# Moving all tiles of a DMA-bound matmul kernel to multiples of 512 B in SBUF

## The chip, the cores and the metric

One core of one Trainium2 chip. The metric is the device time of one execution in microseconds, median of several; a profiled execution gives the trace, whose span runs from the first to the last instruction and is some 1.9 us shorter than the time. Runs that a ratio compares ran on the same chip in alternating rounds, and all of them were in the fast state (no run was over 1.5% above the fastest of its kernel). A ratio is the mean time of one kernel's runs over the mean of the other's of the same rounds, so it is not quite the ratio of the medians beside it.

## The reference

```python
batch, m, k, n = 16, 512, 512, 512          # a: [16, 512, 512], b: [16, 512, 512], float32
def reference(a, b):
    return np.matmul(a.transpose(0, 2, 1), b).astype(np.float32)
```

Each execution reads 33.55 MB and writes 16.78 MB.

## The kernel before

Two batches make a pair; there are 8 pairs. A partition takes 8 rows of K, which lie one after another in HBM: an input tile is 128 partitions x 16 KB, loaded as one run of 16 KB for each partition. An output tile holds two runs of 8 KB for each partition. One issuing engine (SP) queues all 16 loads and then 8 stores. A mark is a write of one element after a piece of work, which raises the semaphore that another engine waits for.

```python
x_ts = [pool.tile([P, R, M], f32, name=f"x{j}") for j in range(NX)]        # 4 input tiles, 16 KB a partition
abf_ts = [pool.tile([P, RV, M], bf, name=f"abf{v}") for v in range(V)]     # 2 + 2 bf16 tiles, 4 KB
bbf_ts = [pool.tile([P, RV, N], bf, name=f"bbf{v}") for v in range(V)]
o_ts = [pool.tile([P, G, T, N], f32, name=f"o{j}") for j in range(NO)]     # 7 output tiles, 16 KB
dve_done = pool.tile([1, 2 * pairs], f32, name="dve_done")                 # marks
act_done = pool.tile([1, pairs], f32, name="act_done")
# ... semaphores ...
for n in range(2 * pairs):
    if n >= NX:
        nc.sync.wait_ge(s_in, n - NX + 1)
    nc.sync.dma_start(x_ts[n % NX][:], in_v[n % 2][n // 2]).then_inc(s_x[n % NX], 16)
for i in range(pairs - 1):
    nc.sync.wait_ge(s_out, i + 1)
    nc.sync.dma_start(out_v[i], o_ts[i % NO][:]).then_inc(s_o if i else s_o0, 16)
# ... DVE casts x to bf16 and sets a mark, PE multiplies, ACT copies PSUM to o and sets a mark ...
# ... the last store is issued after all this ...
```

In the compiled program the first input tile starts at byte 16512 of a partition, which is 128 B past a multiple of 512 B. Since all tiles ahead of the marks are multiples of 512 B long, each of them is 128 B off.

## Time and profile before

| what | before |
|---|---|
| time, median of 3 | 124.13 us (123.99 to 124.22) |
| span | 122.2 us |
| DMA share of the span | 97.6% of 16 engines |
| PE, DVE, ACT busy | 62.9, 38.0, 31.8 us |

The lines of the profile stand in the prediction below, with how to read each. Two measures are used throughout. The views show GB/s in a stretch of the span. Finer, the trace records when each of the 16 DMA engines raises a transfer's semaphore; I call the mean of the 16 times the landing (the prediction's times of landings are those of the last of the 16), and the spacing of successive landings is the pace of the queue. A transfer of a whole tile is always 2.097 MB. A packet is one run that one DMA engine moves, here of 16, 8 or 2 KB, and the trace has its start and duration.

### The profile page before, as it was taken

What the parts mean: (1) busy time and instruction counts of PE and PEld (TensorE: products, weight loads), DVE (VectorE), ACT (ScalarE), POOL (GpSimd) and SP (SyncE); (2) the same over time, 40 slices, a digit from 0 to 9 for tenths busy, and PEclk for the clock granted to TensorE, in tenths of its full rate; (3) what the DMA queues carried; (4) which work ended last, traced back from release to release, by engine and by line L of the source; (5) the groups of instructions that cost most, each with busy time, mean ns of one, the idle gap of its engine ahead of it and who ended that gap; (6) DMA issues with size and microseconds to landing.
All of it is one profiled execution on the core that took longest, in us unless ns stands there. A gap on an engine that the chain in (4) does not pass through costs nothing. (4 is left out here: it accounts for less than half of the span.)

```text
span 122.2 us, 1261 instructions
## 1 busy us (share of the span) xinstructions
PE 62.9 (51%) x512; PEld 35.9 (29%) x512; DVE 38.0 (31%) x48; ACT 31.8 (26%) x41; POOL 0.2 (0%) x4
## 2 busy tenths in 40 slices
PE   0000099989669749969919987955970000000000
PEld 0000044546346314536605545624630000000000
DVE  0012560784194092474456248409000000000000
ACT  4000000380930830191480065092084000000000
POOL 0000000000000000000000000000000000000000
PEclk9999999999999976999996899999999655555555
DMA  4899999999999999999999999999999999999993
GB/s 97 376 440 429 440 435 429 429 429 429 429 429 429 429 429 429 424 435 418 429 424 429 429 429 424 429 400 429 429 427 429 429 427 429 424 429 429 427 429 166
DMA packets 4480, 50.33 MB, mean 412 GB/s; under 512 B 384, under 2 KB 384, under 8 KB 384
## 3 DMA queue, kind: packets, MB, share of 16 engines
q1 hardware_dynamic: 4480, 50.33, 97.6%
HBM read 33.55 MB, written 16.78 MB: 412 GB/s over the span
## 5 line engine op out<-in xcount | busy, mean ns | idle before, releaser
L101 PE MATMUL ps<-bbf,abf 64*128 64x512 bf16 x512 | 62.9, 404 | 27.9 <-PEq L96 27.9
L101 PEld LDWEIGHTS ps<-bbf,abf 64*128 64x128 bf16 x512 | 35.9, 114 | 54.4 <-issue 38.3
L119 ACT COPY o<-ps 128x1024 f32<-128x1024 f32 x32 | 30.1, 1026 | 60.2 <-PE ps L101 60.2
L80 DVE CAST abf<-x 128x2048 bf16<-128x2048 f32 x16 | 19.6, 1224 | 27.0 <-PE ps L101 18.2
L80 DVE CAST bbf<-x 128x2048 bf16<-128x2048 f32 x16 | 19.6, 1225 | 20.7 <-DMA x<-in_b_dram 20.7
L124 ACT ACTIVATE act_done<-act_done 1x1 uint32<-1x1 uint32 x8 | 1.6, 196 | 0.0
L119 ACT ACT_TABLE_LOAD x1 | 1.3, 1283 | 0.9 <-SPq L62 0.9
L86 DVE MEMSET dve_done<- 1x1 f32 x16 | 0.9, 59 | 0.0
L146 POOL MEMSET const-bfloat16-1.0<- 128x1 bf16 x1 | 0.1, 102 | 0.0
L146 POOL MEMSET const-uint8-127<- 128x1 uint8 x1 | 0.1, 102 | 0.0
L146 POOL MEMSET const-float32-0.0<- 128x1 f32 x1 | 0.1, 99 | 0.2 <-issue 0.2
L146 POOL MEMSET const-float32-1.0<- 128x1 f32 x1 | 0.1, 99 | 0.0
## 6 DMA issues: line engine op xcount, KB each, us to landing
x<-in_a_dram SPq DMA_DIRECT2D x8, 2048.0 KB, 12.2
x<-in_b_dram SPq DMA_DIRECT2D x8, 2048.0 KB, 16.0
out_dram<-o SPq DMA_DIRECT2D x8, 2048.0 KB, 30.8
```

Of the source, the lines that this page charges most:

```text
L80: nc.vector.tensor_copy(out=(bbf_ts if n % 2 else abf_ts)[v][:], in_=x_ts[n % NX][:, v * RV:(v + 1) * RV, :],).then_inc(s_cast, 1)
L86: nc.vector.memset(dve_done[:, n:n + 1], 0.0).then_inc(s_in, 1)
L101: mm = nc.tensor.matmul(ps_ts[g][h][:, t % 2, :], a_m[:, t], bbf_ts[v][rows, r, :], start=(v == 0 and r == 0), stop=(v == V - 1 and r == R ...
L119: ev = nc.scalar.copy(out=o_ts[i % NO][:, g, 2 * h:2 * h + 2, :], in_=ps_ts[g][h][:])
L124: nc.scalar.memzero(act_done[:, i:i + 1]).then_inc(s_out, 1)
L146: nc = _bacc.Bacc("TRN2", target_bir_lowering=False, num_devices=1)
```

## The change

The intent is to have all input and output tiles start at multiples of 512 B. The two small tiles of marks become one tile of 384 B at the front, which puts the first input tile at byte 16896 and every tile behind it at a multiple of 512 B.

```diff
+    done = pool.tile([1, 96], f32, name="done")
+    dve_done, act_done = done[:, 0:2 * pairs], done[:, 2 * pairs:3 * pairs]
     x_ts = [pool.tile([P, R, M], f32, name=f"x{j}") for j in range(NX)]
     abf_ts = [pool.tile([P, RV, M], bf, name=f"abf{v}") for v in range(V)]
     bbf_ts = [pool.tile([P, RV, N], bf, name=f"bbf{v}") for v in range(V)]
     o_ts = [pool.tile([P, G, T, N], f32, name=f"o{j}") for j in range(NO)]
-    dve_done = pool.tile([1, 2 * pairs], f32, name="dve_done")
-    act_done = pool.tile([1, pairs], f32, name="act_done")
```

## The prediction

> **What bounds the kernel now.** I read the slices of the page first, then the queue's total, then the groups and the waits, then the timeline for a rate that can be read off to 0.1%. The slices of the page of the kernel before:
>
> ```profile
> span 122.2 us, 1261 instructions
> ...
> DMA  4899999999999999999999999999999999999993
> GB/s 97 376 440 429 440 435 429 429 429 429 429 429 429 429 429 429 424 435 418 429 424 429 429 429 424 429 400 429 429 427 429 429 427 429 424 429 429 427 429 166
> DMA packets 4480, 50.33 MB, mean 412 GB/s; under 512 B 384, under 2 KB 384, under 8 KB 384
> ## 3 DMA queue, kind: packets, MB, share of 16 engines
> q1 hardware_dynamic: 4480, 50.33, 97.6%
> ```
>
> From the third slice (6 us) to the last but one every slice is full and moves about 429 GB/s. No stretch in the middle has the DMA engines waiting for anything. The other rows of the same page:
>
> ```profile
> PE 62.9 (51%) x512; PEld 35.9 (29%) x512; DVE 38.0 (31%) x48; ACT 31.8 (26%) x41; POOL 0.2 (0%) x4
> ...
> x<-in_a_dram SPq DMA_DIRECT2D x8, 2048.0 KB, 12.2
> x<-in_b_dram SPq DMA_DIRECT2D x8, 2048.0 KB, 16.0
> out_dram<-o SPq DMA_DIRECT2D x8, 2048.0 KB, 30.8
> ```
>
> No compute engine is busy for more than 51% of the span. The 24 transfers are of 2.097 MB each; each takes 12 to 31 us from issue to landing because others stand ahead of it in the queue. The waits say who pays:
>
> ```profile
> DVE bbf L80 <- DMA x<-in_b_dram: 20.7, 8, 3.6
> ...
> SPq L157 <- DMA out_dram<-o: 27.7, 1, 27.7
> ```
>
> The casts wait for loads, and at the end all that is left is a 27.7 us wait for stores. The chain of waits ends with compute at 93 us and accounts for only 8% of the span; that is because it can't follow a queue of transfers, and it must not be read as "nothing bounds it". The timeline gives the rate of the loads, since the cast of each b tile starts as its load lands:
>
> ```profile
> 13.64 1.23 DVE L80 CAST bbf<-x 128x2048 bf16<-128x2048 f32 x1 [3.65 <-DMA x<-in_b_dram]
> ...
> 82.18 1.23 DVE L80 CAST bbf<-x 128x2048 bf16<-128x2048 f32 x1 [3.35 <-DMA x<-in_b_dram]
> ```
>
> Between these two are 14 loads: (82.18 - 13.64) / 14 = 4.896 us for one load, 428 GB/s. The last load lands at 82.2 us, so the first two thirds of the span are 16 loads and the rest 8 stores: 82.2 + 8 x 4.89 = 121.3, plus 0.9 us to the end of the span. The semaphore records of the trace give the same more finely: loads land 4.894 us apart (8.75 to 82.16 us, 15 steps), stores 4.886 us apart (91.94 to 116.37 us, 5 steps). The kernel is bound by 24 x 4.89 = 117.4 us of DMA in one queue, and 4.9 us lie around it (start of the first transfer at 2.0 us, some 1.9 us lost on the first packets, which took up to 1.75 us each, and 0.9 us at the end).
>
> **What the Trainium skill says.** (1) The page "DMA: Bandwidth & Descriptors", section "Where 436 GB/s comes from": 16 ports x 32 B x 850 MHz = 435.2 GB/s. At that rate a transfer takes 2,097,152 B / 435.2 GB/s = 4.819 us. The trace shows 4.89, 98.5% of it, so it agrees as a ceiling. (2) The same page, "How a descriptor splits into AXI transactions": data goes in transactions of 256 B and beats of 32 B, and a transaction must start at a multiple of 256 B, so a run that starts off it pays for beats it doesn't use. In the compiled program of the kernel before, four constants of 32 B slots stand ahead of the first input tile, which begins at byte 16512 = 32 x 512 + 128. All input and output tiles are multiples of 512 B long, so every one begins 128 B past such a boundary: 4 beats. (3) The same page, "Why small descriptors are slow (HBM only)": about 3 cycles of overhead for each packet. The packet records behind the page's third section fit well: loads are 2048 packets of 16 KB with a median near 611 ns (12 to 30 us), stores 2048 packets of 8 KB at 309 ns. In cycles of 1/850 MHz = 1.176 ns, 611 ns is 519 = 512 beats + 4 + 3, and 309 ns is 263 = 256 + 4 + 3. That is just what a start 128 B off would cost, though a fixed overhead of 7 cycles for whatever other reason would fit as well. (4) The page "SBUF — State Buffer", section "Operand start alignment", demands only a start at a multiple of the element size and says that it is about legality and not speed. Nothing there makes 512 B a threshold.
>
> **The change part by part.** (a) One tile of 384 B takes the place of two of 64 and 32 B and moves to the front. 16512 + 384 = 16896 = 33 x 512, so all input, bf16 and output tiles move by 384 B and begin at multiples of 512 B. No instruction, wait, transfer or byte is added or removed; the marks are written by the same 16 memsets of 59 ns and 8 activations of 196 ns, into different columns. Both engines now write the same tile, but inside a section with hand-made semaphores, where I expect no new wait. Cost: 0. (b) Casts, matmuls and copies read and write at moved addresses. Their durations shouldn't change, and they aren't on the path: the last store is issued at 93.1 us and its packets start after 116.4 us, 23 us of slack. Worth: 0. (c) Loads: each of the 16 engines carries 8 packets of 16 KB per load, 8 x 16 = 128 in all. If the writes into SBUF lose 4 beats each, it is 128 x 4 x 1.176 ns = 0.60 us. (d) Stores: 16 packets of 8 KB per engine and store, 16 x 8 = 128: again 128 x 4.7 ns = 0.60 us.
>
> Whether (c) and (d) are really paid is seen better from the spacing of the landings than from the packets' durations, since neighbouring packets may overlap. One transfer has 131,072 B per engine, 4096 beats. A load takes 4.894 us = 4160 cycles: 64 over the beats. A store takes 4.886 us = 4153 cycles: 57 over. With 3 cycles for each data packet, a store's 16 packets take 48, and 9 remain for its semaphore packet (9 ns in the records, about 8 cycles). So the stores' spacing is explained without any misalignment, and their 309 ns must overlap by some 4 cycles. A load's 8 packets with the same overhead take 24 + 9 = 33, and 31 cycles are left: 4 for each packet. So the loads seem to pay for the misalignment and the stores seem not to. This is where I chose: (c) in full, (d) not. Sum: 124.13 - 0.60 = 123.53 us, 123.5.
>
> **The rivals.** *Nothing changes:* the 31 cycles of the loads come from reading HBM, or are part of a 16 KB packet whatever its address, and the skill's rule is written for reads, where the loads' reads from HBM are presumably aligned already. For: loads and stores are within 0.2% of each other though one writes SBUF and the other reads it. Against: the overheads come out at whole packets' 4 beats. Time: 124.1. *Both pay:* stores read SBUF, which is the side that the rule describes, and 309 ns fits it; with the overlap gone the spacing of stores could fall by 4 beats as well. Time: 122.9. *More than the sum:* a 512 B boundary could matter for some other reason, in the first packets as well (1.9 us lost there). But at the ceiling of 435.2 GB/s the 24 transfers would take 115.7 us, 1.7 us less than now, which is 1.4%: more than 2% (below 121.65 us) would need a rate above that ceiling or a start without loss. Nothing in the trace speaks for it. *Slower:* the two engines' marks in one tile bring a wait, or the aligned tiles collide in SBUF. With compute 23 us ahead at the end, and a queue that holds about three loads ahead (12 to 16 us from issue to landing, 4.9 us each), a wait of some 100 ns on a mark would be hidden. Time: 124.1 to 124.3.
>
> **Range and chances.** I give the loads alone 0.42, nothing 0.30, both 0.18, more 0.06, slower 0.04. Executions spread by 0.1 us either way. The range from 122.8 to 124.25 us holds the first three with their spread, which is more than 8 in 10; the middle is 123.5. Faster by over 2% has 0.04, slower by over 2% 0.01, the rest is within 2%: 0.95.
>
> **What would show it.** If (c) is right, packets of 16 KB fall from 611 to about 606 ns, the casts of b tiles stand 4.856 us per load apart rather than 4.896, the last load lands near 81.6 rather than 82.2 us, and the slices between 10 and 80 us show about 432 rather than 429 GB/s. If (d) is paid after all, stores stand 4.85 us apart rather than 4.886; if packets of 8 KB go from 309 to 305 ns with the spacing unchanged, the overlap is what hid it. If "nothing changes" is right, both spacings stay to 0.005 us and the seven cycles are a packet's own. The groups of casts, matmuls and copies should keep their means (1225, 404, 1026 ns), and the wait for stores at the end its 27.7 us within 0.5. I'm wrong about the kind of the effect if the span changes by more than 1.7 us, if the gain lies ahead of the first landing (8.8 us), or if a new wait on the marks shows.

## The result, and the profile after

| | before | after |
|---|---|---|
| time, median of 6 | 124.10 us (123.99 to 124.44) | 123.89 us (123.68 to 124.08) |
| ratio | | 0.9978, 95% interval 0.9963 to 0.9994 |
| span of the profiled run | 122.2 us | 121.9 us |

The change is worth 0.22%, 0.27 us. That is clear of noise; the sum of the prediction had said 0.60 us.

The slices and the queue on the page of the changed kernel:

```profile
span 121.9 us, 1261 instructions
...
GB/s 108 360 430 430 436 430 430 430 430 430 430 430 430 430 430 436 430 430 430 430 430 430 430 430 430 436 390 428 428 430 430 430 428 430 430 430 428 428 428 175
...
q1 hardware_dynamic: 4480, 50.33, 97.6%
```

In the loads (slices 4 to 26) most slices have 430 where they had 429; slice 27, where loads give way to stores, has 390 against 400. Everything else is as it was: the same packets, the same bytes, casts of 1225 ns, copies of 1026 ns, no new wait. The wait of the issuing engine for the last stores, in the view of its waits:

```profile
SPq L159 <- DMA out_dram<-o: 27.8, 1, 27.8
```

The timeline has the casts that start when the first and the last b tile land:

```profile
13.67 1.23 DVE L82 CAST bbf<-x 128x2048 bf16<-128x2048 f32 x1 [3.60 <-DMA x<-in_b_dram]
...
81.79 1.23 DVE L82 CAST bbf<-x 128x2048 bf16<-128x2048 f32 x1 [3.34 <-DMA x<-in_b_dram]
```

(81.79 - 13.67) / 14 = 4.866 us for a load, where it was 4.896. So 14 loads gained 0.42 us, but the end came only 0.3 us earlier. The view of busy time by stretch shows where the rest went. Its columns are the stretch, its length, the busy time of the five compute engines (with instructions), the granted TensorE clock, the DMA engines' share and GB/s. Before:

```profile
10.00:64.00 54.00, 39.89 (x320) 22.09 (x320) 25.17 (x32) 19.09 (x25) 0.00 (x0) 0.97 1.01 429
...
78.00:82.00 4.00, 3.02 (x29) 1.73 (x24) 0.83 (x1) 2.70 (x3) 0.00 (x0) 1.00 0.98 414
...
100.00:120.00 20.00, 0.00 (x0) 0.00 (x0) 0.00 (x0) 0.00 (x0) 0.00 (x0) 0.50 1.01 428
```

After:

```profile
10.00:64.00 54.00, 39.69 (x322) 22.09 (x324) 25.51 (x33) 19.10 (x25) 0.00 (x0) 0.97 1.01 431
...
78.00:82.00 4.00, 2.64 (x26) 1.43 (x21) 0.66 (x2) 3.08 (x4) 0.00 (x0) 1.00 0.98 403
...
100.00:120.00 20.00, 0.00 (x0) 0.00 (x0) 0.00 (x0) 0.00 (x0) 0.00 (x0) 0.50 1.01 429
```

The loads are faster, the end of the loads is slower (403 against 414 GB/s), the late stores are the same. The packet records explain the middle line: before, no 16 KB packet after the start of the kernel lasted over 625 ns; after, 11 packets between 78.6 and 80.5 us lasted 646 to 1064 ns. The shortest of the other packets did not become shorter: they last 611 ns in both, though before they strayed up to 624 (mean 613.8) and now nearly all are at 611.

My theory at this point: each packet that goes to or from SBUF off a boundary costs some 4 cycles, the loads' part of it is gained, and part of that is given back where loads turn into stores. The rivals: the two profiles differ by chance; or what counts is bytes or the 512 B boundary rather than packets; or aligned output tiles slow the stores.

### The profile page after: what moved, and what is told of

Its sections match the earlier page's. It is cut to its first block, busy times and chain, and to the rows that moved or that the text cites. A ratio compares the mean times of both kernels' runs of the same rounds, so it can differ in the third digit from the quotient of the medians.

```text
span 121.9 us, 1261 instructions
## 1 busy us (share of the span) xinstructions
PE 62.5 (51%) x512; PEld 35.8 (29%) x512; DVE 38.0 (31%) x48; ACT 31.8 (26%) x41; POOL 0.2 (0%) x4
## 5 line engine op out<-in xcount | busy, mean ns | idle before, releaser
L121 ACT COPY o<-ps 128x1024 f32<-128x1024 f32 x32 | 30.1, 1026 | 59.8 <-PE ps L103 59.8
L82 DVE CAST bbf<-x 128x2048 bf16<-128x2048 f32 x16 | 19.6, 1225 | 20.8 <-DMA x<-in_b_dram 20.8
L126 ACT ACTIVATE done<-done 1x1 uint32<-1x1 uint32 x8 | 1.6, 196 | 0.0
L88 DVE MEMSET done<- 1x1 f32 x16 | 0.9, 59 | 0.0
```

Of the source, the lines that this page charges most:

```text
L82: nc.vector.tensor_copy(out=(bbf_ts if n % 2 else abf_ts)[v][:], in_=x_ts[n % NX][:, v * RV:(v + 1) * RV, :],).then_inc(s_cast, 1)
L88: nc.vector.memset(dve_done[:, n:n + 1], 0.0).then_inc(s_in, 1)
L121: ev = nc.scalar.copy(out=o_ts[i % NO][:, g, 2 * h:2 * h + 2, :], in_=ps_ts[g][h][:])
L126: nc.scalar.memzero(act_done[:, i:i + 1]).then_inc(s_out, 1)
```

## The experiments

### Both kernels again, and each half of the change alone

`before_again` and `after_again` are the two kernels unedited. `x_only` puts 384 B of marks ahead of the input tiles and 128 B ahead of the output tiles; `o_only` puts the 384 B between the bf16 tiles and the output tiles. (In `x_only` the bf16 tiles move along with the input tiles; no DMA touches them.)

```diff
 # x_only, against the kernel before
+dve_done = pool.tile([1, 96], f32, name="dve_done")
 x_ts = [...]                                          # now at 0 mod 512
 ...
+act_done = pool.tile([1, 32], f32, name="act_done")
 o_ts = [...]                                          # still at 128 mod 512
-dve_done = pool.tile([1, 2 * pairs], f32, name="dve_done")
-act_done = pool.tile([1, pairs], f32, name="act_done")
```

```diff
 # o_only, against the kernel before
 x_ts = [...]                                          # still at 128 mod 512
 ...
+act_done = pool.tile([1, 96], f32, name="act_done")
 o_ts = [...]                                          # now at 0 mod 512
 dve_done = pool.tile([1, 2 * pairs], f32, name="dve_done")
-act_done = pool.tile([1, pairs], f32, name="act_done")
```

> The kernel before, unedited, for a second profile. If the spacings of the landings are properties of the kernel, loads land 4.895 us apart and stores 4.887 us apart within 0.004 us, the 16 KB packets again last 611 to 619 ns with a mean of 613.8, and the ratio is 1.000 within 0.002. If the two profiles at hand differ by chance, loads or stores shift by 0.01 us or more here.

> The changed kernel, unedited, for a second profile. If the loads' gain is real: loads 4.862 us apart within 0.004 us, every 16 KB packet at 611 ns. If the stores' loss (4.896 us apart against 4.887) comes from the alignment, it is there again; if it is chance, stores are at 4.887 to 4.890. If the slow packets of 650 to 1060 ns at 78.6 to 80.5 us belong to the change they come again there; if not, the last load lands near 81.6 us and the span is near 121.7. Ratio 0.9978 by the earlier rounds, 0.996 if the slow packets were chance.

> Only the input tiles begin at multiples of 512 B; the output tiles begin 128 B past one as before. Loads alone matter: loads 4.862 us apart, stores 4.887, ratio 0.9955 to 0.998, at least as fast as the changed kernel. If the output tiles' alignment were what costs the stores 9 ns each, this is 0.07 us faster than the changed kernel; if alignment does nothing and the profiles differ by chance, 4.894 and a ratio of 1.000.

> Only the output tiles begin at multiples of 512 B; the input tiles stay 128 B past one. If only loads pay for the offset: loads 4.895 us apart, stores 4.887, ratio 1.000 within 0.001. If aligned output tiles slow the stores: stores 4.896, ratio 1.0006. If stores pay for the offset too (the second rival of the prediction): stores 4.85, ratio 0.9975.

Measured, five rounds on one chip, with the landings of each profile (us, the first two kernels' earlier profiles ahead):

```
kernel        time    ratio (95%)               14 steps, load 1 to 15   last load   last load to last store
before                                          68.516                   4.896       39.096
before_again  124.04  0.9997 (0.9984 to 1.0010) 68.519                   4.896       39.091
o_only        124.02  0.9997 (0.9984 to 1.0010) 68.519                   4.896       39.099
after                                           68.053                   5.010       39.219
after_again   123.89  0.9983 (0.9970 to 0.9996) 68.055                   5.080       39.223
x_only        123.87  0.9988 (0.9975 to 1.0001) 68.053                   4.975       39.226
```

The view by stretch of the two halves, first `x_only`, then `o_only`:

```profile
10.00:64.00 54.00, 39.35 (x322) 22.20 (x324) 25.41 (x33) 18.36 (x24) 0.00 (x0) 0.97 1.01 432
...
78.00:82.00 4.00, 4.00 (x40) 2.56 (x36) 1.42 (x2) 1.46 (x2) 0.00 (x0) 1.00 0.97 403
```

```profile
10.00:64.00 54.00, 39.00 (x320) 22.71 (x320) 25.09 (x32) 19.08 (x25) 0.00 (x0) 0.97 1.01 430
...
78.00:82.00 4.00, 4.00 (x40) 2.36 (x38) 1.23 (x1) 1.25 (x2) 0.00 (x0) 1.00 0.98 414
```

The profiles of each class agree to a few nanoseconds, so nothing here is chance except the size of the last load's delay. The six fall into two classes, and what sorts them is the input tiles alone. With aligned inputs 14 steps of loads take 0.465 us less (4.862 against 4.895 us a load in the steady part; the 4.862 is a mean of steps that repeat in fours, from 4.84 to 4.89 us, which was not looked into), the last load takes 0.08 to 0.18 us more, and from there to the last store it takes 0.13 us more. The sum, -0.465 + 0.126 (mean) + 0.127 = -0.21 us, is what the times show (-0.15 to -0.27; the interval of `x_only` just takes in no change). The loss in the stores does not come from the output tiles: with only those aligned nothing changes at all, and with only the inputs aligned the loss is whole. My expectation of 4.887 us per store for `x_only` was wrong. That loss sits in the first stores: before, their first steps are 4.878, 4.861 and 4.881 us, after, 4.907, 4.900 and 4.899; from the fifth on both stand near 4.89 to 4.90. (Here the first step is that from the first store to the second.)

### Small packets: loads of 2 KB

The saving is small because there are few packets. If it is one of packets, eight times as many must show eight times as much. Each input tile is loaded by two transfers, of its even and its odd rows, so that every row is a run of 2 KB; both operands are permuted alike and the result stays correct. `ld2k_off` has this on the kernel before, `ld2k_on` on the changed kernel.

```diff
-nc.sync.dma_start(x_ts[n % NX][:], in_v[n % 2][n // 2]).then_inc(s_x[n % NX], 16)
+for w in range(2):
+    nc.sync.dma_start(
+        x_ts[n % NX][:, w * 4:(w + 1) * 4, :], in_v[n % 2][n // 2][:, w::2, :]
+    ).then_inc(s_x[n % NX], 16)
 ...
-nc.vector.wait_ge(s_x[n % NX], 16 * (n // NX + 1))
+nc.vector.wait_ge(s_x[n % NX], 32 * (n // NX + 1))
```

> Loads cut into packets of 2 KB: each input tile comes by two transfers, of the even and of the odd rows, so that a row of 2 KB is a run of its own (both operands alike, so the sums are the same). Tiles 128 B past a multiple of 512 B. 64 packets per engine and load where there were 8. With 3 cycles of overhead and 4 beats for the offset each: 64 x (64 + 3 + 4) = 4544 cycles and some 16 for two semaphore packets, 5.36 us per load. If the offset's cost is one of bytes and not of packets, 64 x 67 + 32 + 16 = 4336 cycles, 5.10 us.

> The same with all tiles at multiples of 512 B. If each packet saves the 3.5 to 4 beats that the 16 KB packets saved: 64 x 67 + 16 = 4304 cycles, 5.06 us per load, 0.26 to 0.30 us less than with the offset, and 4.2 to 4.8 us over the 16 loads. If the saving is one of bytes: 0.03 us per load and 0.5 us in all, as in the change.

To find the boundary and the law, three more kernels differ from `ld2k_on` only in the size of the marks' tile, which puts all tiles at 64, 192 or 256 B past a multiple of 512 B (448, 576 or 128 B in place of 384). All five are slower than the kernel before (ratios 1.028 to 1.065), since a load now has eight times the packets; they are compared with each other.

> Loads in packets of 2 KB, all tiles 64 B past a multiple of 512 B. Aligned it was 5.13 us per load (both halves), at 128 B 5.42. If the offset costs the beats between the boundary and the start, 2 for 64 B: 5.28 us per load, 2.2 us of span over the aligned one (130.0 us). If it costs one more transaction whatever the offset: 5.42 us, as at 128 B (132.2 us).

> The same, all tiles 256 B past a multiple of 512 B. If the boundary that counts is 256 B, as the skill's page has it: 5.13 us per load, 127.8 us, as aligned to 512 B. If it is 512 B: 5.42 us per load or more, 132.2 us or more.

> Loads in packets of 2 KB, all tiles 192 B past a multiple of 512 B. At 64 and 128 B the span was 132.1 us, at 0 and 256 B 127.8 us. If each packet that starts off a multiple of 256 B costs the same whatever the distance: 5.42 us per load, 132.1 us. If 192 B costs 6 beats: 5.57 us per load, 134.4 us.

The view by stretch, first `ld2k_on` (0 B past), then `ld2k_at256`, then `ld2k_off` (128 B), `ld2k_at64`, `ld2k_at192`:

```profile
10.00:80.00 70.00, 50.82 (x400) 29.58 (x402) 31.94 (x42) 22.89 (x30) 0.00 (x0) 0.93 1.05 409
```

```profile
10.00:80.00 70.00, 47.90 (x410) 28.43 (x412) 32.23 (x42) 22.91 (x30) 0.00 (x0) 1.00 1.05 409
```

```profile
10.00:80.00 70.00, 51.24 (x384) 27.51 (x384) 29.18 (x38) 20.81 (x27) 0.00 (x0) 0.90 1.05 387
```

```profile
10.00:80.00 70.00, 50.10 (x384) 27.75 (x384) 29.17 (x38) 22.31 (x29) 0.00 (x0) 0.93 1.05 387
```

```profile
10.00:80.00 70.00, 50.49 (x384) 27.94 (x384) 29.17 (x38) 22.91 (x30) 0.00 (x0) 0.93 1.05 387
```

The last column takes one of two values: 409 GB/s at 0 and 256 B, 387 at 64, 128 and 192 B. The times and the spacing of the half tiles' landings say the same more finely:

```
B past 512   time     half tile
0            127.78   2.566 us
256          127.91   2.566
64           132.11   2.711
128          132.18   2.710
192          132.17   2.710
```

The kernels at 0 and 128 B ran on one chip, those at 256 and 64 B on another, that at 192 B (two runs) on a third; the half tiles' spacing agrees to 1 ns within each group. So 4.40 us (3.4%) are lost or gained by the start address alone. A half tile has 32 packets per engine: (2.710 - 2.566) / 32 = 4.5 ns each, 3.8 of the cycles of 1.176 ns that the prediction counts in. The packets' own durations agree: 84.0 ns on average at 0 and 256 B, 88.2 to 88.8 ns at the other three. For the 16 KB packets it is (4.895 - 4.862) / 8 = 4.1 ns, 3.5 cycles. The saving is one of packets; saving by bytes is refuted. The boundary is 256 B; 512 B as such has no effect. And the cost doesn't grow with the distance from the boundary: 64 and 192 B cost what 128 B costs, where a cost by unused beats would have given 130.0 and 134.4 us. A run of 2 KB that starts off a boundary touches 9 blocks of 256 B in place of 8, whatever the distance. That one block more is a fit to these numbers, not a thing that a record shows.

These five kernels also repeat, on three other chips, the loss in the stores (of 8 KB packets here as before): from the last load to the last store it is 39.22 us at 0 and 256 B and 39.10 to 39.11 at 64, 128 and 192 B.

### Small packets: stores of 2 KB

`st2k_off` and `st2k_on` are the kernel before and the changed one with output rows dealt to the partitions in another order, so that a store's runs are of 2 KB (64 packets per engine and store in place of 16).

```diff
-out_v = out.rearrange("(pair g) (c t) n -> pair c g t n", g=G, t=T)
+out_v = out.rearrange("(pair g) (t c) n -> pair c g t n", g=G, t=T)
 ...
-a_m = abf_ts[v][rows, r, :].rearrange("p (c t) -> p t c", t=T)
+a_m = abf_ts[v][rows, r, :].rearrange("p (t c) -> p t c", t=T)
```

> Stores cut into packets of 2 KB (output row t x 128 + c instead of 4 c + t sits in partition c, the columns of the first operand are taken to match, so the result is the same); loads as before. Tiles 128 B past a multiple of 512 B. 64 packets per engine and store where there were 16: with 3 cycles each, 64 x 67 + 9 = 4297 cycles, 5.06 us per store, if the offset costs stores nothing; 64 x 71 + 9 = 4553 cycles, 5.36 us, if it costs them 4 beats. Loads 4.895 us apart.

> The same with all tiles at multiples of 512 B. If stores pay nothing for the offset, stores stand as far apart as with it, within 0.02 us, and only the loads gain, 0.5 us in all. If they pay 4 beats for each packet, each store is 0.30 us shorter, 2.4 us over the 8. If an aligned output tile makes stores slower by packet, they are 9 x 4 = 36 ns longer each.

The stretch of the late stores, off and on:

```profile
95.00:120.00 25.00, 0.00 (x0) 0.00 (x0) 0.00 (x0) 0.00 (x0) 0.00 (x0) 0.50 1.04 396
```

```profile
95.00:120.00 25.00, 0.00 (x0) 0.00 (x0) 0.00 (x0) 0.00 (x0) 0.00 (x0) 0.50 1.05 409
```

Measured: 127.12 us off, 125.91 us on (ratios 1.023 and 1.013 to the kernel before; the profiled runs took 127.12 and 125.79 us). The stores take 42.17 us from the last load off, 41.17 on; another 0.4 us come from the loads. So stores pay as well where packets are small: the six later steps average 5.290 us off and 5.103 on, 0.187 us for 64 packets, 2.9 ns each. That lies between what "nothing" and "4 beats" had let expect, and it is a mean of two kinds of steps. The first three after the first store show no cost (5.064, 5.089, 5.128 us off; 5.122, 5.059, 5.126 on); the last four average 5.380 us off and 5.108 on, 4.3 ns a packet, and in the last three of these the packets themselves last 88.2 to 88.5 ns off and 84.0 on. That stores pay nothing for the offset, as the prediction had chosen, does not hold in general.

### A gap between loads and stores

Why then do stores of 8 KB show nothing, and what are the slow packets of the last load? Both point to the moment when the queue changes direction. One line keeps the two apart: the first store is issued only when all input tiles have been cast. That costs a gap of some 5 us in which the DMA engines run empty (from 81.6 to 86.6 us in `delay_off`); the comparison is among kernels with the gap. The first pair ran on one chip, the second on another.

```diff
+nc.sync.wait_ge(s_in, 2 * pairs)
 for i in range(pairs - 1):
     nc.sync.wait_ge(s_out, i + 1)
```

`delay_off` is the kernel before with it, `delay_on` the changed one, `delay_x_only` and `delay_o_only` have only inputs or only outputs aligned.

> The kernel before, with the first store issued only after all input tiles have been cast, so that no store stands in the queue behind the last loads. That opens a gap of some 4 to 5 us, so it is slower by that. Loads 4.895 us apart to the last. If the shorter steps of the first stores (4.86 to 4.88 us, against 4.896 later) come from stores starting while the last loads drain, all steps are 4.89 to 4.90 here. If they come from the input tiles' addresses as such, they stay.

> The changed kernel with the same gap. If the slow packets of the last load (0.05 to 0.18 us longer in four runs with aligned inputs, none in four without) come from the stores waiting behind it in the queue, they are gone and the last load takes 4.862 us. If they belong to the last load itself, or to that moment, the last load takes 4.94 to 5.08 us again. Against the run with the gap and the offset the gain would be 16 x 0.033 = 0.5 us if both give-backs go with the gap, 0.3 if they stay.

> The gap before the first store, input tiles aligned, output tiles 128 B off. If the 4.98 us per store seen with the gap and the offset is the output tiles' own cost: stores 4.97 to 4.98 us apart, loads 4.862, 129.5 us. If it follows the input tiles: 4.89 us, 128.8 us.

> The gap, input tiles 128 B off, output tiles aligned. If the cost is the output tiles' own: stores 4.89 us apart, loads 4.895, 129.3 us. If it follows the input tiles: 4.98 us, 130.0 us.

The late stores in the view by stretch, in that order:

```profile
95.00:120.00 25.00, 0.00 (x0) 0.00 (x0) 0.00 (x0) 1.14 (x3) 0.00 (x0) 0.52 1.01 420
```

```profile
95.00:120.00 25.00, 0.00 (x0) 0.00 (x0) 0.00 (x0) 0.45 (x2) 0.00 (x0) 0.54 1.02 430
```

```profile
95.00:120.00 25.00, 0.00 (x0) 0.00 (x0) 0.00 (x0) 0.69 (x2) 0.00 (x0) 0.50 1.01 421
```

```profile
95.00:120.00 25.00, 0.00 (x0) 0.00 (x0) 0.00 (x0) 1.01 (x3) 0.00 (x0) 0.50 1.01 429
```

```
kernel         time     load spacing   last load   store spacing (2nd to 8th)
delay_off      130.04   4.895          4.888       4.979
delay_on       128.78   4.862          4.853       4.892
delay_x_only   129.48   4.862          4.853       4.979
delay_o_only   129.32   4.895          4.890       4.893
```

With the gap the two halves come apart cleanly. Loads follow the input tiles, stores follow the output tiles: 0.087 us per store, 5.4 ns for each of its 16 packets, 4.6 cycles. In these late stores the 8 KB packets last 314.8 ns on average with the offset and 309.0 without; in the kernels without the gap they last 309.0 ns in both cases. So behind loads the cost is not hidden by packets that overlap more: neither the packets nor their spacing show it. The last load has no slow packets and is no longer than the others. Alignment is then worth 1.26 us: 0.50 us in 15 steps of loads, 0.61 in seven steps of stores, and the rest between the last load and the first store. This is the prediction's rival "both pay", with both sizes near 4 cycles; but for stores of 8 KB only where they start on idle engines. Neither branch of the expectation for `delay_off` had 4.98 us per store, and none for `delay_on` a gain of more than 0.5 us.

### A store ahead of the last two loads, and a load ahead of the stores

`early_on` is the changed kernel with the first store moved ahead of the 15th load in the queue.

```diff
+if n == 2 * pairs - 2:
+    nc.sync.wait_ge(s_out, 1)
+    nc.sync.dma_start(out_v[0], o_ts[0][:]).then_inc(s_o0, 16)
 nc.sync.dma_start(x_ts[n % NX][:], in_v[n % 2][n // 2]).then_inc(s_x[n % NX], 16)
 ...
-for i in range(pairs - 1):
+for i in range(1, pairs - 1):
```

> The changed kernel with the first store moved ahead of the last two loads in the queue. If the slow packets come wherever a store stands behind a load: there are some at the end of the 14th load, near 69 us, and again at the 16th, and the span is no shorter than that of the changed kernel (ratio to the kernel before 0.998 to 1.000). If they belong to the last loads of the kernel: only there, the same ratio of 0.998. If the early store takes the change of direction off the end: ratio 0.996.

The stretches in which a load is followed by the early store and by the late ones:

```profile
66.00:72.00 6.00, 5.05 (x48) 3.03 (x44) 1.23 (x1) 2.67 (x3) 0.00 (x0) 1.00 0.98 408
78.00:82.00 4.00, 4.00 (x42) 2.29 (x37) 0.00 (x0) 1.33 (x2) 0.00 (x0) 1.00 1.00 426
```

The changed kernel has in the first of these:

```profile
66.00:72.00 6.00, 6.00 (x48) 3.63 (x46) 1.23 (x1) 1.07 (x2) 0.00 (x0) 0.83 1.01 431
```

The dip went to where the store now stands: 408 GB/s in place of 431, with 14 slow packets of 644 to 1095 ns between 68.3 and 70.6 us and three (649 to 773 ns) near 78 us, where there had been 11 up to 80.5. Time 124.14 us, ratio 0.9999 (0.9983 to 1.0016): with two changes of direction more, nothing is left of what alignment had brought. The slow packets belong to a load that has a store behind it.

`again_off` and `again_on` are the kernels with the gap, with one load more (of a tile that isn't used again) between the gap and the stores.

```diff
 nc.sync.wait_ge(s_in, 2 * pairs)
+nc.sync.dma_start(x_ts[0][:], in_v[0][0]).then_inc(s_x[0], 16)
 for i in range(pairs - 1):
```

> The gap, then one load more (of a tile that is loaded a second time and not used again), then the stores queued right behind it; nothing aligned. If the offset's cost to stores (4.98 us per store after the gap) is hidden by standing behind a load, stores are at 4.89 us again. If the gap itself or the time in the run is what shows it, they stay at 4.98.

> The same with all tiles aligned: stores 4.89 to 4.90 us apart in either case. If a store standing behind a load slows the load when inputs are aligned, the extra load has packets of 650 to 1100 ns near its end here and none in the run with the offset.

Measured: 136.42 us off and 136.02 us on, one round each. The stretch of the late stores of the run with the offset:

```profile
100.00:130.00 30.00, 0.00 (x0) 0.00 (x0) 0.00 (x0) 3.23 (x5) 0.00 (x0) 0.50 1.01 428
```

And of the run without:

```profile
100.00:130.00 30.00, 0.00 (x0) 0.00 (x0) 0.00 (x0) 2.66 (x4) 0.00 (x0) 0.50 1.01 428
```

428 GB/s with the offset too, where the gap alone gave 420: the stores are again 4.888 to 4.907 us apart with the offset, and 4.890 to 4.908 without. So with a load right ahead of them the stores do not pay for the offset. What goes with it in all profiles of 8 KB stores is how far the 16 engines are apart: they finish the first store within 0.23 to 0.27 us of each other after a gap, and within 0.49 to 1.03 us behind a load. That the spread is the cause was not tried by itself, and `st2k_off` speaks against a simple form of it: its last four stores pay with the engines 0.69 to 0.91 us apart. The second part of my expectation was a miss: the extra load has slow packets near its end in both runs, with the offset too, so they are not confined to aligned inputs; there the load is the first after a pause and has slow packets at its start as well.

## Why the prediction was right or wrong

The time lay within the range; the gain was 0.27 us where the sum said 0.60. By its own steps:

- What bounds the kernel: right. All of the change is in the queue of transfers; no compute group's mean moved by more than 1 ns, and no new wait on the marks appeared. (What lies around the 117.4 us is 4.8 us by its own parts, not 4.9; nothing rests on it.)
- (a) and (b), nothing from the marks and the engines: right.
- (c) Loads, 0.60 us: that each packet into an offset tile pays is right and was shown by multiplying the packets; the size was a little off. It said 4 beats, 38 ns a load; measured are 33 ns, 3.5 cycles a packet, 0.53 us if all 16 loads gain (the landing of the first, at 8.27 to 8.39 us before and 8.30 to 8.42 after, shows no gain). The reason that it gave is wrong: beats in proportion to the offset would cost 2, 4 and 6 at 64, 128 and 192 B, and all three cost the same. That 4 came near was the luck of a kernel that is 128 B off.
- The step that failed is the sum, which let the loads' saving reach the end whole and set the stores at zero change. Of the 0.53 us, some 0.16 are lost at the last load (0.03 not gained and 0.08 to 0.18 of slow packets), and 0.13 from there to the last store. That leaves 0.24, as measured within its interval. That the loss at the last load needs a store behind it, and the loss in the stores needs aligned input tiles, was shown; why, stays open.
- (d) Stores, 0: right as a net of alignment of the output tiles (`o_only`: 0.9997), wrong as a statement on stores, and so in part luck. They pay 5.4 ns a packet when they start on idle engines and, as packets of 2 KB, 4.3 ns from the fifth store on. The 4.886 us from which it concluded is a mean of the short first steps (4.861 and 4.881 us) and of steady ones of 4.895 to 4.904.
- What the packets' durations would show: wrong. They were to fall from 611 to 606 ns, since 611 and 309 ns had been read as the beats and 4 + 3 cycles. Aligned packets last 611, 309 and, of 2 KB, 84 ns, so those some 7 cycles are a packet's own, as the rival "nothing changes" had it. For 16 KB packets the cost shows in the mean alone (613.8 to 611.0 ns, 2.8 of the 4.1 ns that the landings give). The spacing of landings, predicted at 4.856 us, came to 4.862.
- The ceiling argument against more than 2%: nothing contradicts it; the aligned loads run at 431 GB/s.

What stays open: why the last load slows down when a store stands behind it, some 1.5 to 3 us before the first store's packets are recorded, and why inputs that are off do not show this in the plain kernel; why the first three stores are 0.03 us shorter each behind loads that are off; and what keeps the stores behind loads from paying, all eight of 8 KB but only the first few of 2 KB. No version tried beats the changed kernel: `x_only` is its equal.

## What to carry to other kernels

Start every tile that a DMA touches at a multiple of 256 B: it cost nothing here, and what it brought, where it brought anything, was 4 to 5 ns for each packet, whatever the packet's size: 0.2% with runs of 8 and 16 KB and 3.4% with runs of 2 KB in the loads. When a cost is too small to be seen, multiply the number of times it is paid before you argue about it. And in a queue that is always full, a gain in one stage has to be followed to the end: here half of it was gone at the change from loads to stores.

## What the Trainium skill lacked or had wrong

- "DMA: Bandwidth & Descriptors", section "How a descriptor splits into AXI transactions": the 256 B boundary agrees with the runs (2.566 us a half tile at 0 and at 256 B). Its account of unused beats, which grow with the distance from the boundary, does not describe loads into SBUF: 2.711, 2.710 and 2.710 us at 64, 128 and 192 B. The page tells it for what a transaction reads; the cost when SBUF is written is missing.
- "SBUF — State Buffer", section "Operand start alignment", says that its runs timed nothing. The price by packet was 4.1 ns for loads of 16 KB runs, 4.5 ns for 2 KB, 5.4 ns for stores of 8 KB on idle engines.
- "DMA: Bandwidth & Descriptors", section "Why small descriptors are slow (HBM only)": about 3 cycles per packet. From the aligned loads it is nearer to 4: a full tile takes 4.862 us with 8 packets per engine, a half tile 2.566 us with 32. At 850 MHz these are 37 and 133 cycles over their beats (4096 and 2048), and (133 - 37) / (32 - 8) = 4.0, if nothing else sets the two sizes apart. The aligned stores give 3.7 in the same way (5.103 us with 64 packets, 4.892 with 16).
- No page says that a load into aligned tiles with a store behind it in the same queue slows at its end (packets of 646 to 1064 ns for 611), or that the same stores, 128 B off, run at 4.98 us after a gap and 4.90 us behind a load.
